# Row variance of a 64 MB array on one core: larger loads, no sums on TensorE, and a tapered end

## The chip, the core and the metric

The kernel runs on one core of one Trainium2 chip. The metric is the device time of one execution in microseconds (us). "Span" is the time from the first to the last instruction in the profile; the device time of the same run is about 1.8 us longer. One program on one core has no second die to compare with, so a run counts as slow only if it is over 1.5% above the fastest of its kernel.

## The reference

```python
batch, seq, dim = 32, 512, 1024           # x: float32, 16384 rows of 1024
mean_sq = np.mean(x**2, axis=-1)
sq_mean = np.mean(x, axis=-1)**2
return (mean_sq - sq_mean).astype(np.float32)
```

Each of 128 partitions holds 128 rows. I call one row per partition, 128 x 1024 floats or 0.5 MB, a "column". There are 128 columns, and all 67.1 MB have to be read once.

## The kernel before

There are three ways to get a column's variance, and the kernel mixes them: bn (VectorE, two statistics instructions and one aggregate, which give mean and variance), a sum of squares on ScalarE with the plain sum on VectorE, and a sum of squares on ScalarE with the plain sum on TensorE (eight transposes accumulated in PSUM, the memory that TensorE writes to; a copy out by VectorE; a matmul with ones).

```python
xt_fill = opool.tile([P, 8, D], FP32)          # columns 120..127, loaded first
nc.sync.dma_start(out=xt_fill, in_=col_range(FILL0, 8))
for gi in range(NBODY):                        # 13 stages of 8 columns
    c0 = gi * 8
    nbn, ncl = 3, 2
    xt = xpool.tile([P, 8, D], FP32, name="xt")   # 3 buffers
    nc.sync.dma_start(out=xt, in_=col_range(c0, 8))
    for k in range(nbn):        do_bn_col(xt[:, k, :], c0 + k)
    for k in range(nbn, 8):     do_square_col(xt[:, k, :], c0 + k)      # ScalarE
    nc.vector.reduce_sum(out=pair_stage[:, 0, c0+3 : c0+5], in_=xt[:, 3:5, :], ...)
    do_tensor_cols(xt, [(k, c0 + k) for k in range(5, 8)])              # TensorE
    if 2 <= gi <= 9: do_filler_col(gi - 2)
    # ... combine() for finished columns, first output after gi == 12

for (c0, ncols) in [(104,4),(108,4),(112,2),(114,2),(116,2),(118,1),(119,1)]:
    nc.sync.dma_start(out=xt_end[:, ...], in_=col_range(c0, ncols))
    # columns by "CSAA": ScalarE square + VectorE sum; two ScalarE passes; bn; bn
# ScalarE: square of the sums of columns 104..127; VectorE: subtract; output DMA
```

## Time and profile before

| | before |
|---|---|
| device time, median of 6 | 167.77 us (167.52 to 168.87) |
| span of the profiled run | 166.5 us (this run took 168.29 us, 0.5 more than the median) |
| instructions | 1460, of which 940 on TensorE (470 matmuls, 470 weight loads) |
| stream, 20 to 140 us | 429 GB/s, DMA engines 1.00 busy |

The DMA engines are busy from the first slice to almost the last, and no compute engine is over 64% busy. This is a kernel that streams.

The next view is the timeline of VectorE, before: only those instructions that ended a wait for a load (start, duration, engine, line, operation, and in brackets the wait). Each shows when an 8-column load had landed.

```profile
42.47 1.88 DVE L112 BATCH_NORM_STATS2 stats<-xt 128x6 f32<-128x512 f32 x3 [2.38 <-DMA xt<-in_x_dram]
53.00 1.88 DVE L112 BATCH_NORM_STATS2 stats<-xt 128x6 f32<-128x512 f32 x3 [2.88 <-DMA xt<-in_x_dram]
62.71 1.88 DVE L112 BATCH_NORM_STATS2 stats<-xt 128x6 f32<-128x512 f32 x3 [2.15 <-DMA xt<-in_x_dram]
...
82.15 1.88 DVE L112 BATCH_NORM_STATS2 stats<-xt 128x6 f32<-128x512 f32 x3 [2.15 <-DMA xt<-in_x_dram]
93.10 1.88 DVE L112 BATCH_NORM_STATS2 stats<-xt 128x6 f32<-128x512 f32 x3 [3.39 <-DMA xt<-in_x_dram]
...
141.69 1.88 DVE L112 BATCH_NORM_STATS2 stats<-xt 128x6 f32<-128x512 f32 x3 [2.40 <-DMA xt<-in_x_dram]
```

Subtract neighbours. 53.00 to 62.71 is 9.71 us, and so are nine other intervals within 0.03 us. But 42.47 to 53.00 is 10.53, and 82.15 to 93.10 is 10.95. Two loads came 0.8 and 1.2 us late, and the stream never made it up. An average over the whole stage hides that; the differences between landings show it.

The timeline of the last microseconds, before:

```profile
162.18 1.23 DVE L112 BATCH_NORM_STATS2 stats<-xt_end 128x6 f32<-128x512 f32 x2
...
163.44 0.21 DVE L115 BATCH_NORM_AGGREGATE pair_stage<-stats 128x2 f32<-128x12 f32 x1
163.75 0.22 ACT L221 ACTIVATE sqm_stage<-pair_stage 128x24 f32<-128x24 f32 x1 [1.15 <-DVE pair_stage L115]
164.00 0.17 DVE L230 TENSOR_TENSOR pair_stage<-msq_stage,sqm_stage 128x12 f32<-128x12 f32 x1 [0.35 <-ACT sqm_stage L221]
164.20 0.35 SPq L237 DMA_DIRECT2D out_dram<-pair_stage  x1
```

The last column is a whole one: two statistics and an aggregate, then a square on ScalarE and a subtraction on VectorE, then the output DMA at 164.20.

### The profile page before, as it was taken

The numbers are of one execution on the slowest core, as the hardware profiler recorded it, in microseconds if no ns is written. First come the engines' busy times: TensorE is split into PE (matmuls) and PEld (weight loads), VectorE is DVE, ScalarE is ACT, GpSimd is POOL, SyncE is SP. The second block draws the span as 40 slices with busy tenths as digits, with TensorE's granted clock in tenths as the row PEclk, the third lists the DMA queues.
The fourth block names the chain that finished last, engine by engine and source line by source line (L and its number), as shares of the span: only waits on it lengthen the run. The fifth ranks groups of instructions, "written<-read, shape, count | busy, mean of one in ns | idle before, by whom it ended". The sixth has DMA issues, their size and how long they took to land.

```text
span 166.5 us, 1460 instructions
## 1 busy us (share of the span) xinstructions
PE 83.6 (50%) x470; PEld 79.4 (48%) x470; DVE 107.1 (64%) x230; ACT 99.7 (60%) x175; POOL 0.7 (0%) x7
## 2 busy tenths in 40 slices
PE   0000048393792959557492674929567391950000
PEld 0000047392792949457492664929566381940000
DVE  0000049395793949759394694949769393999993
ACT  3000049192782948759394694939767291998981
POOL 1000000000000000000000000000000000000000
PEclk9999999758567596978969698696957659576555
DMA  6999999999999999999999999999999998999920
GB/s 213 417 457 425 433 433 409 457 409 457 425 445 433 411 449 401 451 425 433 394 405 457 409 441 425 425 457 409 453 417 441 433 435 382 429 413 425 410 112 3
DMA packets 3319, 67.26 MB, mean 404 GB/s; under 512 B 624, under 2 KB 624, under 8 KB 880
## 3 DMA queue, kind: packets, MB, share of 16 engines
q1 hardware_dynamic: 3168, 67.12, 94.7%
q10 hardware_dynamic: 144, 0.05, 0.1%
q8 instruction: 3, 0.05, 0.1%
q14 instruction: 4, 0.03, 0.1%
HBM read 67.11 MB, written 0.07 MB: 403 GB/s over the span
## 4 chain that ended last, share of the span: by engine, by line
DMA 70%; DVE 28%; issue 0%; SPq 0%; ACT 0%; ACTq 0%
DMA xt<-in_x_dram 70%; DVE stats L112 16%; DVE pair_stage L171 7%; DVE pair_stage L206 3%; DVE pair_stage L115 2%; DVE folded L142 0%; SPq L79 0%; ACT sqm_stage L221 0%; SPq L165 0%; DVE pair_stage L230 0%; DVE pair_stage L102 0%; DVE pair_stage L152 0%; ACTq L221 0%
## 5 line engine op out<-in xcount | busy, mean ns | idle before, releaser
L118 ACT ACTIVATE scratch<-xt 128x1024 bf16<-128x1024 f32 x65 | 68.7, 1057 | 60.2 <-DMA xt<-in_x_dram 58.6
L133 PE MATMUL psum_f<-ident,xt 128*128 128x128 f32 x312 | 63.9, 397 | 54.5 <-DMA xt<-in_x_dram 54.5
L133 PEld LDWEIGHTS psum_f<-ident,xt 128*128 128x128 f32 x312 | 59.9, 214 | 55.4 <-DMA xt<-in_x_dram 32.3
L112 DVE BATCH_NORM_STATS2 stats<-xt 128x6 f32<-128x512 f32 x78 | 48.8, 667 | 51.0 <-DMA xt<-in_x_dram 51.0
L171 DVE TENSOR_REDUCE pair_stage<-xt 128x2 f32<-128x2048 f32 x13 | 29.5, 2271 | 0.0
L143 PEld LDWEIGHTS psum_s<-ones,folded 128*128 128x128 f32 x94 | 11.5, 191 | 13.9 <-DVE folded L142 13.9
L143 PE MATMUL psum_s<-ones,folded 128*128 128x1 f32 x94 | 12.4, 252 | 10.7 <-DVE folded L142 10.7
L118 ACT ACTIVATION_READ_ACCUMULATOR scratch<-xt 128x1 f32 x65 | 12.1, 186 | 0.0
L112 DVE BATCH_NORM_STATS2 stats<-xt_end 128x6 f32<-128x512 f32 x16 | 10.1, 667 | 0.0
L142 DVE COPY folded<-psum_f 128x128 f32<-128x128 f32 x47 | 9.9, 269 | 0.1
L115 DVE BATCH_NORM_AGGREGATE pair_stage<-stats 128x2 f32<-128x12 f32 x47 | 9.3, 197 | 0.1
L118 ACT ACTIVATE scratch<-xt_end 128x1024 bf16<-128x1024 f32 x8 | 8.5, 1057 | 1.1 <-DMA xt_end<-in_x_dram 0.9
L133 PE MATMUL psum_f<-ident,xt_fill 128*128 128x128 f32 x64 | 9.0, 288 | 0.0
L118 ACT ACTIVATE scratch<-xt_fill 128x1024 bf16<-128x1024 f32 x8 | 8.5, 1057 | 0.3
L133 PEld LDWEIGHTS psum_f<-ident,xt_fill 128*128 128x128 f32 x64 | 8.2, 155 | 0.0
L152 DVE COPY pair_stage<-psum_s 128x3 f32<-128x3 f32 (+1 forms) x21 | 3.3, 159 | 5.2 <-PE psum_s L143 4.7
L206 DVE TENSOR_REDUCE pair_stage<-xt_end 128x1 f32<-128x1024 f32 x4 | 4.7, 1185 | 0.0
L213 ACT ACTIVATE scratch<-xt_end 128x1024 bf16<-128x1024 f32 x4 | 4.2, 1056 | 0.1
L118 ACT ACT_TABLE_LOAD x1 | 1.3, 1283 | 0.7 <-PEq L254 0.7
L118 ACT ACTIVATION_READ_ACCUMULATOR scratch<-xt_end 128x1 f32 x8 | 1.5, 186 | 0.0
L118 ACT ACTIVATION_READ_ACCUMULATOR scratch<-xt_fill 128x1 f32 x8 | 1.5, 186 | 0.0
L83 ACT ACTIVATE sqm_stage<-pair_stage 128x64 f32<-128x64 f32 (+2 forms) x3 | 0.7, 228 | 0.7 <-DVE pair_stage L152 0.7
(12 smaller groups left out, 2.7 us busy)
## 6 DMA issues: line engine op xcount, KB each, us to landing
xt<-in_x_dram SPq DMA_DIRECT2D x13, 4096.0 KB, 23.8
xt_fill<-in_x_dram SPq DMA_DIRECT2D x1, 4096.0 KB, 12.6
xt_end<-in_x_dram SPq DMA_DIRECT2D x2, 2048.0 KB, 29.7
xt_end<-in_x_dram SPq DMA_DIRECT2D x3, 1024.0 KB, 36.1
xt_end<-in_x_dram SPq DMA_DIRECT2D x2, 512.0 KB, 24.1
out_dram<-pair_stage ACTq DMA_DIRECT2D x1, 52.0 KB, 6.6
out_dram<-pair_stage SPq DMA_DIRECT2D x1, 12.0 KB, 1.4
```

The costliest lines, as they stand in the source:

```text
L83: nc.scalar.activation(out=sqm_stage[:, c0 : c0 + n], in_=pair_stage[:, 0, c0 : c0 + n], func=mybir.ActivationFunctionType.Square, scale=1 ...
L112: nc.vector.bn_stats(out=stats[:, s, :], in_=xcol[:, s * FMAX : (s + 1) * FMAX])
L115: nc.vector.bn_aggr(out=pair_stage[:, :, i], in_=stats)
L118: nc.scalar.activation(out=scratch, in_=xcol, func=mybir.ActivationFunctionType.Square, scale=inv_sqrt_d, accum_out=msq_stage[:, i : i + 1],)
L133: nc.tensor.matmul(out=psum_f, lhsT=xt[:, k, ch * P : (ch + 1) * P], rhs=ident, is_transpose=True, start=(ch == 0), stop=(ch == DCH - 1),)
L142: nc.vector.tensor_copy(out=folded, in_=psum_f)
L143: nc.tensor.matmul(out=psum_s[:, slot : slot + 1], lhsT=folded, rhs=ones, start=True, stop=True,)
L152: nc.vector.tensor_copy(out=pair_stage[:, 0, i0 : i0 + nt], in_=psum_s[:, :nt])
L171: nc.vector.reduce_sum(out=pair_stage[:, 0, c0 + nbn : c0 + nbn + ncl], in_=xt[:, nbn : nbn + ncl, :], axis=mybir.AxisListType.X,)
L206: nc.vector.reduce_sum(out=pair_stage[:, 0, i : i + 1], in_=xcol, axis=mybir.AxisListType.X,)
L213: nc.scalar.activation(out=scratch, in_=xcol, func=mybir.ActivationFunctionType.Copy, accum_out=pair_stage[:, 0, i : i + 1],)
```

## The change

The intent is fewer, larger loads, no TensorE work, and an end in which little work is left after the last byte. The diff, cut to its core:

```diff
-    # 13 loads of 8 columns, 8 filler columns first; 3 of every 8 summed on TensorE
-    end_plan = [(104,4),(108,4),(112,2),(114,2),(116,2),(118,1),(119,1)]
+WHOLE = [   # (buffer of 16 columns, columns in this load, columns on ScalarE)
+    (0,16,6),(1,16,6),(2,16,6),(3,16,6),(4,16,6),
+    (5,13,5),(6,11,4),(7,8,2),(6,5,2),(5,3,1),(7,3,1),(7,2,1),(7,1,1)]
+PIECES = [(126,0,512),(126,512,512),(127,0,512),(127,512,256),(127,768,256)]
...
+    for step, (t, n, na) in enumerate(WHOLE):
+        nc.sync.dma_start(out=xt[:, k*D:(k+n)*D], in_=src(c, n))
+        if n == 16:
+            for j in range(4): bn_column(...)          # VectorE
+            split_columns(xt, k + 4, c + 4, 12)        # 12 ScalarE squares, ONE VectorE sum of 12
+            continue
+        # bn for n - na columns; two ScalarE passes (square, copy) for na columns
+        # combine on GpSimd
+        if step == 5:
+            nc.scalar.dma_start(out=out_pc[:, 0:80], in_=mv[:, 1, 0:80])
+    # PIECES: one bn_stats for each piece as it lands, one aggregate per column
```

ScalarE's throw-away output also moves from bf16 in SBUF to float32 in PSUM.

## The prediction

> **What bounds the kernel now.** The input is 67.1 MB. The table of windows shows 425 to 439 GB/s in every 20 us stretch from 20 to 140 us with the DMA engines 0.99 to 1.02 busy, so the stream is saturated. The Trainium skill ("DMA: Bandwidth & Descriptors", section "Bandwidth", Where 436 GB/s comes from) gives 435 GB/s as the ceiling; the trace agrees, 98% of it. The chain of waits is 70% DMA, 28% VectorE. VectorE is on it only at the end: column 112 lands at 141.7 us, VectorE is then busy without a gap until 163.6, though the data has all landed by about 160.3 (DMA share 0.14 in 160 to 161 us, 0 after). The last subtract ends at 164.2; output DMA and exit take 2.3 more: span 166.5. So all but the last 4 to 6 us are the stream. TensorE (83.6 us) and ScalarE (99.7 us) are not the limit.
>
> **What the change does.** The stream keeps its bytes and its queue; loads become 16 columns (8 MB) in three 64 KB buffers, then taper 13, 11, 8, 5, 3, 3, 2, 1 columns, two halves, a half and two quarters. All TensorE work and its PSUM copies go. Per 16 columns VectorE does 4 bn columns and one reduction of 12; the tail has 31 bn columns on VectorE and 17 columns of two ScalarE passes; small combines move to GpSimd.
>
> Costs from the trace: one bn column advances the chain by 1.26 us; the reduction costs 1.06 ns per element ((2271-1185)/1024), so 12 columns 13.1 us (estimate); one ScalarE pass with its accumulator read repeats every 1.18 us. A 16-column stage costs VectorE 18.2 us, ScalarE 14.2, against 19.8 us of stream (1.236 us per column between landings at 23.0 and 141.7). So compute keeps up, buffers come free with about 20 us of transfers queued, and the stream should not starve.
>
> **Critical path after.** Nothing is gained before column 112 lands: about 141.7 again. From there VectorE has 16 bn columns, 20.2 us, plus 0.3 for the last column's third piece and waits: 162.1. Before, it needed 22.3 us there. ScalarE is as close: its first output DMA stands in its queue ahead of column 80's stage and waits for VectorE's fifth reduction (120.3) and three GpSimd operations, to about 121.7; then 34 passes end at 161.8, and GpSimd at about 162.3. Last data about 160.2. Output and exit 2.3: span about 164.5, 2 us less. Time minus span was 1.3 to 1.8 us, so the time is about 165.6 us.
>
> Predicted: 165.6 us, 8 in 10 between 163.9 and 167.0. Faster by over 2% (under 164.4): 0.17; within 2%: 0.81; slower: 0.02.
>
> **What would show it right or wrong.** Page: PE busy 0; VectorE about 130 us, ScalarE about 111; GB/s per slice unchanged near 428 until the last 6 us. Chain of waits: DMA, then bn statistics or ScalarE passes continuous from about 142 to 148 us on. DMA share 0.9 or more until then. Last data to output DMA: under 2.5 us, against 4 now.
>
> **What would make it wrong.** Larger descriptors moving the stream rate: 1% is 1.6 us. ScalarE's scratch now in PSUM: the skill ("ScalarE: Activation LUTs", section "Step-by-step: what each stage is for") calls PSUM the lower-latency destination; no trace here shows it yet, and shorter passes would leave VectorE alone on the chain. GpSimd operations over 1 us each would hold ScalarE back. If the slowest DMA engine lags more with 8 MB loads, landings and the tail come later.

## More of the kernel before

From the page of the kernel before: busy times, the DMA rows of the 40 slices, the DMA queues, and the chain of work that ended last.

```profile
span 166.5 us, 1460 instructions
...
PE 83.6 (50%) x470; PEld 79.4 (48%) x470; DVE 107.1 (64%) x230; ACT 99.7 (60%) x175; POOL 0.7 (0%) x7
...
DMA  6999999999999999999999999999999998999920
...
q1 hardware_dynamic: 3168, 67.12, 94.7%
...
q8 instruction: 3, 0.05, 0.1%
q14 instruction: 4, 0.03, 0.1%
...
DMA 70%; DVE 28%; issue 0%; SPq 0%; ACT 0%; ACTq 0%
```

Note two small lines: q8 and q14 carry *instructions*, not data. Three packets on q8 move 0.05 MB.

## The result, and the profile after

| | before | after |
|---|---|---|
| device time, median | 167.78 us (16 runs) | 165.64 us (8 runs) |
| ratio | | 0.9868 (95% interval 0.9851 to 0.9885) |
| span of the profiled run | 166.5 us | 163.9 us |
| instructions | 1460 | 471 |

A ratio here is the mean time of one kernel's fast runs over that of the other's in the same rounds, so it is not quite the ratio of the medians. The predicted time was 165.6 us. The number is right. The steps that led to it are not all right.

The page after, the same parts:

```profile
span 163.9 us, 471 instructions
...
DVE 130.6 (80%) x159; ACT 109.3 (67%) x189; POOL 6.6 (4%) x35
...
DMA  8969979998997997998998899999999999999970
...
q1 hardware_dynamic: 2736, 67.13, 95.8%
q10 hardware_dynamic: 144, 0.04, 0.1%
q14 instruction: 3, 0.02, 0.0%
...
DMA 73%; DVE 24%; POOL 0%; issue 0%; SPq 0%; POOLq 0%
```

VectorE at 130.6 us and ScalarE at 109.3 are as forecast, and TensorE is gone. The line of q8 is gone too.

VectorE's waits for loads after the change. The loads of the first four lines are 16 columns each; at 139.76 the same 112 columns have landed as at 141.69 before.

```profile
42.54 1.88 DVE L98 BATCH_NORM_STATS2 stats<-xt 128x6 f32<-128x512 f32 x3 [1.29 <-DMA xt<-in_x_dram]
61.90 1.88 DVE L98 BATCH_NORM_STATS2 stats<-xt 128x6 f32<-128x512 f32 x3 [1.33 <-DMA xt<-in_x_dram]
81.38 1.88 DVE L98 BATCH_NORM_STATS2 stats<-xt 128x6 f32<-128x512 f32 x3 [1.45 <-DMA xt<-in_x_dram]
100.91 1.88 DVE L98 BATCH_NORM_STATS2 stats<-xt 128x6 f32<-128x512 f32 x3 [1.50 <-DMA xt<-in_x_dram]
...
139.76 1.88 DVE L98 BATCH_NORM_STATS2 stats<-xt 128x6 f32<-128x512 f32 x3 [0.65 <-DMA xt<-in_x_dram]
```

The intervals are 19.36, 19.48 and 19.53 us for 16 columns: no late load as large as those before. The last microseconds, after:

```profile
160.73 0.19 POOL L122 TENSOR_TENSOR sqm<-mv 128x1 f32<-128x1 f32 x1 [1.90 <-ACT scratch L111]
161.01 0.19 POOL L123 TENSOR_TENSOR mv<-msq,sqm 128x1 f32<-128x1 f32 x1
161.07 0.24 DVE L196 BATCH_NORM_AGGREGATE mv<-stats 128x2 f32<-128x18 f32 x1
161.38 0.35 SPq L198 DMA_DIRECT2D out_dram<-mv  x1
```

GpSimd (behind ScalarE's last pass) and VectorE finish within 0.11 us of each other, at 161.20 and 161.31.

### A finer look: sixteen landings for each load

The Trainium skill ("DMA: Bandwidth & Descriptors", section "Why a DMA increments its semaphore by 16 and not by 1") says that a load is spread over up to 16 DMA engines that finish independently, and that only the full count of 16 means that all data has landed. The trace has these increments with their times, and it agrees: every load here has sixteen, at different times. From them I read, for each load, when the first and when the last engine was done. (These are times from the trace's semaphore records, in us; the waits above show only the last engine.)

```
                        column 112 landed          last load landed        output DMA
run              q8     first    last    gap       first    last    gap    issued
before            3     138.75  141.66   2.91      158.60  161.50   2.90   164.20
after             0     138.67  139.74   1.07      158.64  160.15   1.51   161.38
```

The *first* engine is as fast in both kernels. What differs is how far the *slowest* engine has fallen behind it: 2.9 us before, 1.1 to 1.5 us after. Once grown, the gap stays: before, it is 1.64 to 1.65 us for four loads in a row and then 2.89 to 2.91 for six. A delay of one engine is thus a delay of every later load, and nothing evened it out while the queue was full.

In the kernel before, the gap of single loads was 0.82 us when 32 columns had landed (42.44 minus 41.62) and 1.64 at column 40 (52.98 minus 51.34). Between the two, at 48.51 us, lies the first q8 packet: 16 KB, 1.01 us long, and a 32 KB data packet that begins at 49.51, where the q8 packet ends, takes 1764 ns where such packets take 1213. Sorted, the sixteen engines lag behind the first of them by (us):

```
32 columns  0.00 0.07 0.09 0.12 0.17 0.20 0.21 0.24 0.25 0.33 0.48 0.49 0.61 0.63 0.75 0.82
40 columns  0.00 0.07 0.08 0.17 0.20 0.20 0.24 0.25 0.32 0.46 0.49 0.60 0.62 0.75 0.81 1.64
```

Fifteen of them keep their places; one goes from 0.12 to 1.64. The 1.52 us that it lost are the q8 packet and the longer data packet, 1.01 + 0.55. In the seven fetches of the kernel before, b_newtail and a_pe_many (both told of below) that no other disturbance overlaps, one engine lost 1.50 to 1.55 us each time. The third q8 packet, at 116.91, left the gap at 2.9, because the engine that it met was not the slowest: it went from 0.48 to 2.02. (The trace does not name a packet's engine; that the packet and the late engine belong together is read from the times.) The second q8 packet, at 83.94, lies in the other long interval, but not alone: from 80.0 to 81.2 us eight data packets took 1.9 to 2.4 us instead of 1.2, and the next load has seven engines 1.5 us or more behind the first, where the one before it had one. How the 1.2 us of this interval divide between the two is not shown.

In the two profiled runs the span differs by 2.60 us. That is more than the 2.14 us between the medians, because the profiled run of the kernel before was a slow one (168.29 us). Counted at the last load: it landed 1.35 us earlier (161.50 to 160.15); the output DMA was issued 1.23 us after it instead of 2.70, which is 1.47 us; and the exit took 0.22 us longer (2.30 to 2.52). But in neither kernel does VectorE wait for the last load. From column 112 on VectorE works through its backlog and is idle for 0.3 us in all after the change and 0.5 before, so what counts is when column 112 lands and how much work is left then:

```
from the landing of column 112 to the output DMA, us
old end:                       before 22.54   b_nope 22.64
new end, old body:             b_newtail 23.06   b_nope_newtail 23.05
new end, new body (a_* below): after 21.63   a_ctrl 21.47   a_outsp 21.53   a_pe_many 21.47
                               a_pe_few 21.49   a_split8 21.62   a_split8b 21.68   a_split4 21.68
```

Counted so, the 2.60 us are 1.92 for the earlier landing of column 112 (141.66 to 139.74) and 0.90 for a shorter end, less the 0.22 of the exit.

### The profile page after: what moved, and what is told of

Read it like the earlier page. It is cut to its first block, busy times and chain, and to the rows that moved or that the text cites. A ratio compares the mean times of both kernels' runs of the same rounds, so it can differ in the third digit from the quotient of the medians.

```text
span 163.9 us, 471 instructions
## 1 busy us (share of the span) xinstructions
DVE 130.6 (80%) x159; ACT 109.3 (67%) x189; POOL 6.6 (4%) x35
## 4 chain that ended last, share of the span: by engine, by line
DMA 73%; DVE 24%; POOL 0%; issue 0%; SPq 0%; POOLq 0%
DMA xt<-in_x_dram 64%; DVE mv L156 16%; DMA out_dram<-mv 9%; DVE stats L98 6%; DVE stats L193 2%; DVE mv L101 0%; DVE mv L196 0%; SPq L166 0%; POOL sqm L133 0%; POOL sqm L137 0%; POOL mv L140 0%; POOLq L140 0%
## 5 line engine op out<-in xcount | busy, mean ns | idle before, releaser
L149 ACT ACTIVATE scratch<-xt 128x1024 f32<-128x1024 f32 x60 | 61.6, 1027 | 44.2 <-DMA xt<-in_x_dram 42.4
L98 DVE BATCH_NORM_STATS2 stats<-xt 128x6 f32<-128x512 f32 x98 | 60.8, 662 | 30.3 <-DMA xt<-in_x_dram 30.3
L156 DVE TENSOR_REDUCE mv<-xt 128x12 f32<-128x12288 f32 x5 | 64.7, 12934 | 0.0
L104 ACT ACTIVATE scratch<-xt 128x1024 f32<-128x1024 f32 x17 | 17.5, 1028 | 5.9 <-DVE stats L98 5.1
L111 ACT ACTIVATE scratch<-xt 128x1024 f32<-128x1024 f32 x17 | 17.5, 1028 | 0.5
L149 ACT ACTIVATION_READ_ACCUMULATOR scratch<-xt 128x1 f32 x60 | 11.2, 186 | 0.0
L101 DVE BATCH_NORM_AGGREGATE mv<-stats 128x2 f32<-128x12 f32 x49 | 9.6, 197 | 0.2
L133 POOL TENSOR_SCALAR sqm<-mv 128x12 f32<-128x12 f32 x5 | 1.2, 237 | 115.2 <-DVE mv L156 115.2
L111 ACT ACTIVATION_READ_ACCUMULATOR scratch<-xt 128x1 f32 x17 | 3.2, 186 | 0.0
L104 ACT ACTIVATION_READ_ACCUMULATOR scratch<-xt 128x1 f32 x17 | 3.2, 186 | 0.0
L122 POOL TENSOR_TENSOR sqm<-mv 128x1 f32<-128x1 f32 (+3 forms) x8 | 1.6, 195 | 37.7 <-ACT scratch L111 37.7
L193 DVE BATCH_NORM_STATS2 stats<-xt 128x6 f32<-128x512 f32 (+1 forms) x5 | 2.7, 568 | 0.0
L123 POOL TENSOR_TENSOR mv<-msq,sqm 128x1 f32<-128x1 f32 (+3 forms) x8 | 1.5, 193 | 0.6
L137 POOL TENSOR_TENSOR sqm<-sqm,mv 128x12 f32<-128x12 f32 x5 | 1.0, 209 | 0.4
```

The source lines that it names most:

```text
L98: nc.vector.bn_stats(out=stats[:, s, :], in_=xcol[:, s * FMAX : (s + 1) * FMAX])
L101: nc.vector.bn_aggr(out=mv[:, :, c], in_=stats[:, 0:2, :])
L104: nc.scalar.activation(out=scratch, in_=xcol, func=ACTF.Square, scale=1.0 / 32.0, accum_out=msq[:, c : c + 1],)
L111: nc.scalar.activation(out=scratch, in_=xcol, func=ACTF.Copy, scale=1.0 / D, accum_out=mv[:, 0, c : c + 1],)
L122: nc.gpsimd.tensor_tensor(out=sqm[:, :n], in0=mean, in1=mean, op=ALU.mult)
L123: nc.gpsimd.tensor_tensor(out=mv[:, 1, c : c + n], in0=msq[:, c : c + n], in1=sqm[:, :n], op=ALU.subtract,)
```

## The experiments

Theory A: the landing gain is the vanished instruction fetches of TensorE's program. Theory B: it is the larger loads. Theory C: it is TensorE's activity itself, its reading of SBUF or its power. Beside them stands the end, which all three leave alone. (Fetches are the DMA packets that bring an engine's instructions.) Runs of one group below ran on one chip with the kernel before beside them; compare ratios, because the three chips' times of the kernel before are 168.28, 167.68 and 167.65 us.

### First group: TensorE's program, its activity, and the size of loads

**b_nope**: the kernel before without TensorE's sums, except in the last stage.

```diff
-        nbn, ncl = 3, 2
+        nbn, ncl = 3, (2 if gi == 12 else 5)      # VectorE sums all 5 columns in one reduction
 ...
-        do_tensor_cols(xt_fill, [(j, i)])
+        nc.scalar.activation(out=scratch, in_=xt_fill[:, j, :], func=Copy, accum_out=...)
```

> The kernel before, with the TensorE sums of stages 0 to 11 replaced by one VectorE reduction of 5 columns (and a second ScalarE pass for the 8 filler columns); the loads and the end are as before, TensorE keeps only stage 12. TensorE instructions fall from 940 to 54. Theory A (instruction fetches of TensorE's program interrupt single DMA engines and the load waits for the slowest engine): the three 16 KB packets of the instruction queue q8 vanish, the landings of successive 8-column loads are 9.7 us apart all through with no interval over 10.2, column 112 lands near 139.8 instead of 141.7, and the time falls by about 1.9 us to about 165.9. Theory B (larger loads are why the stream is ahead): the loads keep their size, so intervals of 10.5 and 10.9 stay, column 112 lands near 141.7 and the time stays near 167.8.

Measured: ratio 0.9958 (0.9939 to 0.9978), so 0.7 us faster, not 1.9. Its page has no q8 line:

```profile
q14 instruction: 3, 0.02, 0.0%
```

Column 112 landed at 141.01, the gap was 1.75 instead of 2.91. Theory A's direction holds, its size does not. The landings had two intervals of 10.1 and 10.3 us although there was no q8 packet. Part of that is another kind of slowdown: from 55.6 to 56.5 us eight data packets took 2.2 to 2.5 us instead of 1.2, and even the first engine lost 0.56 us (61.56 minus 51.29 is 10.27 instead of 9.71). Such bursts appear in most traces, at other times (before: 80.0 to 81.2 us). I did not find their cause, and one profile's landings are uncertain by about half a microsecond because of them.

**a_pe_many** and **a_pe_few**: the changed kernel plus TensorE work that nobody reads, in many short or in few long instructions.

```diff
+        if step <= 5:
+            extra_tensor_work(xt, 16 if n == 16 else 13)
+    # a_pe_many: 5 * n transposes of 128x128, lhsT = xt slice, rhs = ident   (465 in all)
+    # a_pe_few:      n matmuls, lhsT = ident, rhs = xt slice of 512 columns  (93 in all)
```

> The changed kernel plus useless TensorE work whose result nobody reads: 465 transposes of 128x128 (930 instructions), about as many instructions as the kernel before. Theory A (instruction fetch): 16 KB packets of q8 come back, column 112 lands 1 to 2 us later than 139.8, the time is 166.6 to 167.6. Theory C (TensorE's reading of SBUF or its power slows the stream, not its program): also slower here, and slower in the run with few long matmuls too. Theory B: unchanged, 165.6.

> The changed kernel plus useless TensorE work of about the same busy time or more in few instructions: 93 matmuls of 512 columns (186 instructions). Theory A (instruction fetch): no packet of q8 during the run, column 112 lands near 139.8, time within 0.3 us of 165.6. Theory C (TensorE activity itself): slower, 166.6 to 167.6, as in the run with many instructions.

Measured: a_pe_many 0.9904 (0.9887 to 0.9921), a_pe_few 0.9880 (0.9863 to 0.9898); the changed kernel has 0.9868, and 0.9865 as the control below. The instruction queues of a_pe_many:

```profile
q8 instruction: 3, 0.05, 0.1%
q14 instruction: 3, 0.02, 0.0%
```

and of a_pe_few:

```profile
q14 instruction: 3, 0.02, 0.0%
q8 instruction: 1, 0.02, 0.0%
```

The number of q8 packets follows the number of TensorE instructions as the trace counts them: 940 give 3 and 930 give 3, 372 give 1, 60 or none give 0. (The 93 matmuls of a_pe_few became 186 matmuls and 186 weight loads in the trace; the expectation had counted 186 in all, and 54 for b_nope.) TensorE was busy 96.2 us in the one and 93.1 in the other, so activity is equal and the program is not. Many instructions cost 0.6 us, (0.9904 - 0.9867) x 168; few cost 0.2 us, which is within the intervals. The intervals of these two runs overlap a little, so their times alone would not decide between A and C; with the packets and the gaps below they speak for A. I had expected no q8 packet in a_pe_few and was wrong, but that one packet gives a good look at a fetch. It lies at 85.45 us, and the gap of the slowest engine goes from 0.88 us (81.43 minus 80.55) to 1.92 (101.82 minus 99.90) across it and stays there. Up to 81.4 us TensorE had already been busy for 48.4 us without a fetch, and the gap was 0.88 where the control below has 0.83 at the same column. One thing fits theory C: by then even the first engine had lost 0.4 us (39.15 us for the last 32 columns, 38.71 in the control), in a profiled run that is the slowest of its four. In the old body TensorE's work shows no such loss: the first engine takes 9.71 us for 8 columns in the kernel before and 9.72 in b_newtail (below) with it, and 9.71 in b_nope_newtail without.

```
gap between first and last engine when column 112 had landed, us
3 q8 packets:  before 2.91   b_newtail 2.19   a_pe_many 2.19
1 q8 packet:   a_pe_few 1.93
none:          b_nope 1.75   a_outsp 1.28   a_split4 1.25   a_split8 1.22   a_ctrl 1.15
               b_nope_newtail 1.13   a_split8b 1.12   after 1.07   a_best 0.99
```

(The runs in the table that have not been told of yet follow.) The first fetch of a run moved the slowest engine by 0.8 to 1.1 us. Two more add 0 to 0.3 us where no burst falls in with them, because they meet engines that have slack.

**a_split8**: the changed kernel with each 16-column load split into two.

```diff
-        nc.sync.dma_start(out=xt[:, k*D:(k+n)*D], in_=src(c, n))
+        h = 8 if n == 16 else n
+        for o in range(0, n, h):
+            nc.sync.dma_start(out=xt[:, (k+o)*D:(k+o+h)*D], in_=src(c + o, h))
```

> The changed kernel with each 16-column load split into two of 8 columns into the same buffer. Theory A: no more instructions on the compute engines, so column 112 lands near 139.8 as in the changed kernel and the time stays within 0.3 us of 165.6. Theory B (load size): column 112 lands 1 to 2 us later, and the time is 166.6 to 167.6.

Measured: 0.9896, but from 0.9863 to 0.9929, with single times from 165.9 to 167.05. That tells nothing either way; it was repeated in the third group.

### Second group: a control, a larger dose, the output DMA, and an attempt at a better version

**a_ctrl**: the changed kernel again, unedited.

> The changed kernel once more, as the control on this chip. All theories: ratio to before 0.987, within 0.002; no packet of q8; the slowest engine finishes the last load 1.0 to 1.7 us after the first engine, and column 112 between 139.6 and 140.4 us.

Measured: 0.9865 (0.9850 to 0.9880), 165.41 us. Column 112 landed at 139.49, a tenth of a microsecond earlier than the range I gave; the gap at the last load was 1.41.

**a_pe_dose**: the same useless work in 1488 tiny matmuls.

```diff
+        for j in range(n * 16):
+            nc.tensor.matmul(out=junk[0:8, ...], lhsT=xt[:, j*8:(j+1)*8], rhs=ident[:, 0:8], ...)
```

> The changed kernel plus 1488 tiny TensorE matmuls of 8 columns (2976 instructions) that nobody reads. Theory A (instruction fetch interrupts single DMA engines): 10 to 12 packets of 16 KB on q8; the first engine still finishes column 112 near 138.7, the slowest between 141.5 and 145 (in between if the fetches spread over the engines, late if they share one), and the time is 1 to 4 us over the control's. Theory C (TensorE activity, not its program): less TensorE busy time than with 465 transposes, so at most their time, 0.8 us over the control.

Measured: 187.6 us, ratio 1.118. This is far outside what either theory said, and it is a spoilt experiment: each such matmul became two in the trace (2976, with as many weight loads), so 23 q8 packets came instead of 10 to 12, and TensorE itself became the slow engine and held the buffers. The queue waits of SyncE say so:

```profile
SPq L183 <- PE junk L172: 87.2, 5, 23.6
SPq L183 <- DVE mv L161: 57.2, 3, 38.8
```

The loads waited 87.2 us in total for TensorE, and the stream ran dry. Its total time therefore says nothing about A. One reading from before the stream ran dry is of use: at column 80, after 11 fetches, the first engine was on time (99.47; 99.50 in the control) and the slowest at 103.25, a gap of 3.78 against 1.12 in the control. Eleven fetches cost 2.7 us, not eleven times 1.5 us, which fits fetches that spread over several engines.

**a_outsp**: the first output DMA leaves ScalarE's queue.

```diff
-        if step == 5:
-            nc.scalar.dma_start(out=out_pc[:, 0:80], in_=mv[:, 1, 0:80])
+        if step == 12:
+            nc.sync.dma_start(out=out_pc[:, 0:80], in_=mv[:, 1, 0:80])
```

> The changed kernel with its first output DMA moved from ScalarE's queue to SyncE's, behind the last whole-column load. In my prediction ScalarE and VectorE finished together. If VectorE alone holds the end: ScalarE starts column 88 some 3.6 us earlier (about 116.7 instead of 120.2), it waits for data later on, and the time stays within 0.2 us of the control. If ScalarE holds the end too: 0.3 us or more faster.

Measured: 0.9871 (0.9856 to 0.9886), the control's time within the interval. ("Column 88" in the expectation is the stage that starts with column 80.) ScalarE did start that stage earlier, in a_outsp:

```profile
116.86 1.03 ACT L104 ACTIVATE scratch<-xt 128x1024 f32<-128x1024 f32 x1 [1.61 <-DMA xt<-in_x_dram]
```

than after the change:

```profile
120.24 1.03 ACT L104 ACTIVATE scratch<-xt 128x1024 f32<-128x1024 f32 x1 [5.14 <-DVE stats L98]
```

and then waited for data at 130.18 and 139.89 instead. So this blocked queue, which I had counted as ScalarE's part of the critical path, is worth nothing measurable: VectorE finishes at the same time anyway.

**a_best**: as a_outsp, and bn instead of the long sum in stage 4, and finer loads from column 80 on.

```diff
-    (4,16,6), (5,13,5),(6,11,4),(7,8,2),(6,5,2),(5,3,1),(7,3,1),(7,2,1),(7,1,1)
+    (4,16,5), (5,8,3),(5,8,3),(6,8,3),(6,5,1),(6,3,1),
+    (7,3,1),(7,3,1),(7,3,1),(7,2,1),(7,1,0),(7,1,1),(7,1,0)
```

> An attempt to beat both: the output as in the run before this; stage 4 by 11 bn columns and 5 columns of two ScalarE passes instead of the 12-column reduction (VectorE free of it about 4 us earlier); finer loads from column 80 (8, 8, 8, 5, 3, 3, 3, 3, 2, 1, 1, 1 columns). If VectorE's backlog sets the last 1.2 us after the last landing: the last aggregate ends 0.7 us after the last landing instead of 1.2, time 0.3 to 0.7 us under the control. If only the slowest DMA engine counts: no change.

Measured: 0.9889 (0.9872 to 0.9905), 0.4 us slower than the control on the same chip. The backlog did vanish earlier: VectorE waited 0.90 us for data at 150.77 and 0.76 at 157.11. But the last three columns are complete at 157.09, 158.81 and 160.08 us and VectorE needs about 1.4 us for each, so the last aggregate still began 1.2 us after the last landing (160.08 and 161.28). And four more loads cost something, as the next group suggests. No version here beats the changed kernel.

### Third group: the end alone, both parts, and the number of loads

**b_newtail**: the kernel before with the changed kernel's end. **b_nope_newtail**: the same on top of b_nope.

```diff
-    for (c0, ncols) in end_plan: ...          # 16 columns by "CSAA", then square and subtract
+    for off, n, na in [(0,5,2),(5,3,1),(8,3,1),(11,2,1),(13,1,1)]:
+        # one load; bn for n - na columns; two ScalarE passes for na; combine on GpSimd
+    for off, cuts in [(14,(0,512,1024)), (15,(0,512,768,1024))]:
+        # one load and one bn_stats for each piece, then one aggregate
```

> The kernel before with only its last 16 columns done the changed kernel's way: loads of 5, 3, 3, 2 and 1 columns, two halves, a half and two quarters; bn on VectorE, two ScalarE passes on 6 columns, small combines on GpSimd, no final square and subtract. TensorE's work stays, so three q8 packets and a late column 112 (141.2 to 141.9). If end and stream are separate parts of the gain of 2.2 us, this gets the part of the end: 1.2 to 1.6 us, ratio 0.990 to 0.993. If the gain is the stream alone: ratio 0.999 to 1.0.

> Both at once: TensorE's sums taken out of stages 0 to 11, and the new end; the body's loads stay at 8 columns. If the parts add up and load size is worth nothing: ratio 0.985 to 0.989, as the changed kernel's 0.987. If the larger loads bring a part of their own: 0.990 or more.

Measured: b_newtail 1.0038 (1.0025 to 1.0051) and b_nope_newtail 0.9976 (0.9962 to 0.9990). Both missed: the new end alone makes the kernel before 0.6 us *slower*. The last microseconds of b_newtail:

```profile
162.16 0.24 DVE L237 BATCH_NORM_AGGREGATE pair_stage<-stats 128x2 f32<-128x18 f32 x1
162.36 1.06 ACT L211 ACTIVATE scratch<-xt_end 128x1024 bf16<-128x1024 f32 x1
...
163.86 0.19 POOL L224 TENSOR_TENSOR pair_stage<-msq_stage,sqm_stage 128x1 f32<-128x1 f32 x1
164.08 0.35 SPq L241 DMA_DIRECT2D out_dram<-pair_stage  x1
```

VectorE is done at 162.40, 1.39 us after the last landing (161.01), so its part of the new end works. But ScalarE still has a pass to run, and the output goes out at 164.08. ScalarE began its twelve passes of the end only at 149.38, because in this body the square for the combining and the first output DMA stand ahead of them in its queue and wait for VectorE. The old end has twelve passes on ScalarE too, but they began at 147.66, two of them ahead of that square. In the changed kernel these combinings are on GpSimd and the first output has left long before, so that ScalarE is level with VectorE. The new end is therefore not a part that can be bought alone: it needs ScalarE free at column 112. The runs do not give a price for it by itself.

The two runs are also the cleanest pair for theory A, on one chip and with one end. From 1.0038 to 0.9976 is 1.0 us, and the two intervals do not overlap. Column 112 landed at 141.02 in b_newtail, with three fetches, and at 139.80 in b_nope_newtail, without any. There the intervals between the landings of 8-column loads are 9.70 to 9.80 us throughout, which is what theory A had said of b_nope; and 139.80 with 8-column loads is as early as 139.74 with the large loads of the changed kernel.

**a_split8b** and **a_split4**: the 16-column loads split into two (again, with more rounds) and into four (`h = 4` in the diff of a_split8).

> The split of the 16-column loads into 8 columns again, because its first result (0.9896, interval 0.0033 each way) tells neither way. Load size worth nothing: 0.986 to 0.988. Worth half a microsecond: 0.989 to 0.990.

> The 16-column loads split into four of 4 columns: a second dose of the same. Load size worth nothing: 0.986 to 0.988. If 8 columns cost half a microsecond: 0.991 or more here.

Measured: a_split8b 0.9895 (0.9882 to 0.9909), a_split4 0.9939 (0.9927 to 0.9952). Load size is worth something after all: 5 more loads cost 0.5 us and 15 more cost 1.2 us against the control's 0.9865. The reason can be read from the first engine, which no fetch has held up. Its cadence through the five large loads:

```
run         loads   first engine done, columns 16 and 80   us for 16 columns
after          1     22.39   99.81                           19.355
a_split8b      2     22.26   99.98                           19.43
a_split4       4     22.15  100.47                           19.58
```

Each additional load costs 0.075 us on an engine that is always busy, in both doses. (More loads are also smaller pieces for each partition, 32 and 16 KB instead of 64, and these runs do not separate the two.) So theory B was not wrong, only small. The kernel before has 21 loads and the changed one 18, so this part of the gain would be about 0.2 us (an estimate, 3 x 0.075). The profiled pair does not show it: the first engine was done with the last load at 158.60 us before and 158.64 after (158.32 in the control).

## Why the prediction was right or wrong

- **The time**, 165.6 us forecast and 165.64 measured: right by luck. The landing of column 112 was forecast 2.0 us too late and VectorE's work after it 1.05 us too short; the exit took 0.2 us more than the 2.3 forecast. That leaves the forecast span, 164.5 us, 0.6 us too long (163.9 measured). The last step hid it: it added 1.1 us from span to time, where both profiled runs have 1.8 (168.29 less 166.5, 165.69 less 163.9).
- **"Nothing is gained before column 112 lands: about 141.7 again."** This step failed. It landed at 139.74 (139.49 in the control). I had divided 141.7 minus 23.0 by 96 columns and taken 1.236 us per column for the stream's rate. The stream's rate was 9.71 us per 8 columns, 1.214 each, plus two late loads. The late loads were partly fetches of TensorE's instructions, which the change removes. Three comparisons put a price of 0.6 to 1.0 us on them: b_nope (0.7) and b_nope_newtail against b_newtail (1.0) by taking them away from the old body, which also moves sums to VectorE, and a_pe_many (0.6) by giving them back to the new one.
- **"From there VectorE has 16 bn columns, 20.2 us, plus 0.3."** The term was mis-sized: it took 21.55 us (139.76 to 161.31). Within a load the aggregate hides behind the next column's statistics, at 1.26 us a column. At the end of each load it does not, which costs about 0.13 us each time, and the two columns in pieces took 1.62 and 1.48 us with their waits. This error has the other sign, 1.05 us, and cancels half of the first. The old end took 22.5 us, so the new one is shorter, but by 0.9 us and not by the 1.8 us forecast (22.3 less 20.5).
- **"The data has all landed by about 160.3"**, read from the DMA share of the kernel before: wrong by 1.2 us. The last load's sixteenth engine reported at 161.50. Before the change the end was closer to the data than I thought; "about 160.2" for the changed kernel was then right (160.15) for no good reason.
- **ScalarE as close as VectorE:** right in time (GpSimd behind it was done 0.11 us before VectorE, in the control after it), but the blocked output DMA that I gave as its cause is not one: a_outsp took it away and the time stayed.
- **"TensorE is not the limit"**: right about its work, and a trap. Its program was on the path without its work being there.
- **Risk named, "larger descriptors moving the stream rate"**: the direction was right: 0.075 us for each load saved, by the runs that split the loads.
- **PSUM for ScalarE's scratch:** no effect on the time is seen, and no run isolates it. The Trainium skill ("ScalarE: Activation LUTs", section "Step-by-step: what each stage is for") calls PSUM the lower-latency destination. A pass is 1.03 us long instead of 1.06 (its output type changed too), but passes with their accumulator read still repeat every 1.18 us.

What stays open: of the 2.2 us, 0.6 to 1.0 are shown for the fetches by experiment. About 0.7 more, the shorter end less the longer exit (0.9 less 0.2), is read from the traces, where it repeats in eight runs against two; no run isolates it, since b_newtail turned the gain into a wait for ScalarE. The rest, some 0.5 to 0.9 us, is not accounted for; fewer loads (0.2, an estimate) and bursts may have a part in it. The bursts that slow eight or more packets at once are not explained. That successive fetches meet different DMA engines is read from the lags, since the trace does not name the engines.

## What to carry to other kernels

In a kernel that streams at the DMA limit, look at the differences between landings, not at the mean rate: a load is done when its slowest DMA engine is, so one interruption of one engine can delay everything behind it. Instruction fetches are such interruptions (1.5 us of one DMA engine each, here); an otherwise idle engine that does a helper's work in a thousand short instructions is not free. Look also for the last landing that an engine really waits for: here it was column 112, and after it VectorE was idle for 0.3 us in all. And before moving work at the end, check which *other* engine's queue is still full there, because that engine inherits the end.

## What the Trainium skill lacked or had wrong

- No page says what an instruction fetch costs a stream of loads. "Runtime: NRT & Kernel Launch", section "Instruction fetch mechanics", has the fetch itself: 16 KiB blocks of 256 instructions, brought by a DMA queue of the engine's sequencer, at a cost that it calls mostly hidden. The blocks agree: q8 packets of 16,384 bytes, of which 5952, 940, 930, 372 and 60 TensorE instructions gave 23, 3, 3, 1 and 0. The cost was not hidden from the loads: a packet took 0.93 to 1.07 us in all runs but the spoilt one, one DMA engine lost 1.50 to 1.55 us, and the first such packet of a run put the slowest DMA engine 0.8 to 1.1 us further behind (before, a_pe_many, a_pe_few, b_newtail).
- "DMA: Bandwidth & Descriptors", section "Queues, rings and completion order", gives row 14 to the runtime and names refills there. Here 8 KB instruction packets came on q14, but the packets that go with TensorE's program came on q8.
- The same page, section "Bandwidth", has rates of 341 GB/s at 1 MB and 425 GB/s at 16 MB per load, and its rules ask for 1 MiB or more. It has no figure for queued loads: here each additional load in a full queue, with smaller pieces for each partition, cost 0.075 us (first engine's cadence), and 2 MB loads instead of 8 MB loads cost 0.7% of the time.
- The same page, under "Where 436 GB/s comes from", says without condition that for loads from HBM the HBM side, about 358 GB/s, binds; a note a few lines above it keeps that figure for two cores that stream at once. With one core running, the stream held 429 GB/s from 20 to 140 us; the page "HBM Reference" has it right for a core alone.
- "ScalarE: Activation LUTs", section "Step-by-step: what each stage is for": PSUM as destination went with an instruction 29 ns shorter (1057 to 1028 ns; its output type changed too), but passes with an accumulator read kept their interval of 1.18 us.
- No page that I found prices VectorE's batch-norm statistics. Here 128x512 float32 took 662 to 667 ns, and a column of 1024 (two statistics and an aggregate) advanced the engine by 1.26 us.
